# A hybrid decoder layer in one kernel: moving pieces of streamed weights, the group norm and two parameter transposes in TensorE's order

## The chip, the cores and the metric

The kernel runs on one core of a Trainium2 chip. The metric is the device time of one execution in microseconds (us), the median of several executions. Before the change it is 406.03 us.

## What is computed

The reference is one decoder layer on 256 tokens of width 1024. Two mixers share one input projection: RWKV-7 time mixing (8 heads of 64, a recurrence over the tokens) and softmax attention (8 heads of 64; with 256 tokens its blocks come down to plain causal attention). Their outputs are projected, gated, added and projected again; then comes a gated MLP of width 2816.

```
h = rms_norm(x, norm1_g)
proj = h @ w_in                              # recurrence inputs, q/k/v, two gates
z = shifted mix of proj[..., :RWKV_IN] with the token before
y_a = rwkv7_time_mix(z, ...)                 # state = state*w + (state@a)b + v k ; y = state@r
                                             # then a group norm over each head, + bonus, * g
y_b = moba_attention(rope(rms(q)), rope(rms(k)), v)
x = x + (sigmoid(g_a) * (y_a @ w_branch_a) + sigmoid(g_b) * (y_b @ w_branch_b)) @ w_out
x = x + conv_ffn(rms_norm(x, norm2_g), w_up, conv_w, conv_b, w_down)
```

## The kernel before

All large products are done in split form: a weight tile arrives by DMA (`raw`), ScalarE rounds it to a high part (`whi`, L259), VectorE subtracts to get the low part (`wlo`, L269), and TensorE makes three products for each tile (high by high, high by low, low by high). In the input and branch projections (`wst`, L293) one *piece* is 12 such matmuls of 128x256 (L302, L304, L307) and two pieces use up one weight tile. There are three `wlo` buffers, so the next low part can be made when TensorE leaves a tile.

The recurrence works on four chunks of 64 tokens. Within a chunk the delta rule is a triangular system, whose inverse `X` is built from blocks of 16, then 32, then 64: `below` (L791) makes the off-diagonal products, `masked` (L797) masks them into `P`, `plain` (L808) and `turned_` (L818) multiply on, and VectorE adds the results to `X`. Then, chunk by chunk: products with the state (L933, L938), with the inverse (L946), the state update (L956) and the output `y` (L968). `group_norm` takes each chunk's `y`: sum and centring (L892 to L895), square (ScalarE, L896), variance (L898, L899), a power of -1/2 on GpSimd (L900), scaling (L903), two full-size transposes on TensorE into `pc` (L910), and four steps that give the high and low parts `yah` and `yal` (L915 to L918), which the branch projection of the recurrence, `branch(0, *yah)`, reads.

All of these small matmuls use a part of the 128x128 array (64x64, 64x128 or 128x64); streamed pieces and the `pc` transposes use all of it.

The order of the instructions is written by a small planner at the end of `body` (L1174 to L1189). Each thread is a generator: `chain` (recurrence), `gn` (group norm), `att` (attention) and `bulk` (streamed pieces). A thread issues instructions and then yields `(cost, latency)`: the planner's clock advances by the cost, and the thread is due again after the latency. At each step the first thread of the list that is due goes; so the list's order is the priority. `bulk` stands last, costs 1.32 for a piece and has no latency, so it fills whatever time the others leave. `group_norm` holds back its transposes until the last step with a cost was not one of `bulk` (`joined`), so they stand next to other small matmuls. Beyond the threads, after `bulk` has ended, only `branch(0, *yah)`, the output projection and the MLP follow. On VectorE and ScalarE the compiler may let a later instruction go first when an earlier one is not ready by its own estimate; TensorE's order in the trace is the planner's.

The two parameter tables `p1` (51 rows) and `p2` (88 rows) come in by DMA as rows and are turned by TensorE into columns (L158, L1249).

Of the kernel before, what the change touches and what calls it, by code (L numbers as in the profile page):

```python
# [18 lines left out]
S = 256  # L19
# [18 lines left out]
def body(tc, x, positions, norm1_g, w_in, rwkv_mu, w_decay_up, decay_bias, w_aaa_up,  # L38
# [3 lines left out]
    act, dve, pool, pe = nc.scalar, nc.vector, nc.gpsimd, nc.tensor  # L42
    ctx = ExitStack()
    with ctx:
# [19 lines left out]
        def t1(name, shape=(128, 256), dt=F32):  # L64
            return sb.tile(list(shape), dt, name=name, tag="c1", bufs=8)
# [4 lines left out]
        def acc(name="acc"):  # L70
            return ps.tile([128, 512], F32, name=name, tag="acc", bufs=3)

        def chp(name="ch"):
            return ps.tile([128, 512], F32, name=name, tag="ch", bufs=3)

        def atp(name="at"):
            return ps.tile([128, 512], F32, name=name, tag="at", bufs=2)
# [14 lines left out]


        p0 = t1("p0", (8, 128))
        p1 = t1("p1", (51, 128))
        mu1 = rwkv_mu[0]
        rk1 = r_k[0].rearrange("h n -> (h n)").rearrange("(n c) -> n c", c=128)

# [14 lines left out]
        ident = cst.tile([128, 128], F32, name="ident")  # L113
# [41 lines left out]

        def late_params():
            pt = atp("pt")
            pe.transpose(pt[:, 0:51], p1, ident[:51, :51])  # L158
            dve.tensor_copy(par[:, 8:59], pt[:, 0:51])
            dve.tensor_scalar(omm, par[:, MU:MU + 15], -1.0, 1.0, op0=OP.mult, op1=OP.add)  # L160
            dve.tensor_scalar(omka, par[:, KA:KA + 4], -1.0, 1.0, op0=OP.mult, op1=OP.add)
# [60 lines left out]
        def load_next(first=False, into=None):  # L222
            if queue:
                ap = queue.pop(0)
                raw = wp.tile([128, 1024], F32, name="raw", tag="raw", bufs=NRAW) if into is None else into
                if ap is None:

                    nc.sync.dma_start(raw[:, 0:CW], w_gate_up[0, 0:128])
                    for r in range(4):
                        nc.sync.dma_start(raw[32 * r:32 * r + 32, CW:2 * CW], w_gate_up[0, 128:160])  # L230
                    raws.append((raw, 2, CW))
                    return
                k, c = ap.shape[1], ap.shape[2]
                rv = raw[:, :k * c].rearrange("p (k c) -> p k c", k=k)
                for ks in ((slice(0, 2), slice(2, 4)) if first else (slice(0, k),)):
                    nc.sync.dma_start(rv[:, ks], ap[:, ks])
                raws.append((raw, k, c))
# [126 lines left out]
        def first_steps():  # L364
# [5 lines left out]
            for t in early:  # L370
                for i in range(2):
                    load_next(into=t[:, i])
            dve.memset(ones, 1.0)
            dve.memset(eps1[:, 0:1], NORM_EPS)
            dve.memset(eps1[:, 1:2], GN_EPS)
            keep_warm(8)
# [10 lines left out]
            pt = atp("pt")  # L387
# [67 lines left out]
            p = acc()  # L455
# [29 lines left out]
        with tc.manual_schedule(engines={E.PE, E.Activation, E.DVE, E.Pool}):  # L485
            p = first_steps()
# [24 lines left out]
        p = acc()  # L511
# [39 lines left out]
        def need(nm, d):  # L551
            while nm not in d:
                yield 0, 0.5
# [6 lines left out]
        def chain():  # L560
# [36 lines left out]
            p = [chp("pss") for _ in range(2)]  # L597
            for t in range(2):
                for ct in range(4):
                    i = 4 * t + ct  # L600
# [14 lines left out]
            for j in range(2):  # L615
                p = chp("prx").rearrange("p (a t c) -> p a t c", a=2, t=2)
# [163 lines left out]
            def zeros():  # L780
                P = [b2("P", [128, 8, 64]) for _ in range(2)]
                for t in P:
                    pool.memset(t, 0.0)
                return P
# [10 lines left out]
            def masked(P, p, mk, w):  # L795
                m = level(0, w, mk[:, None, :])
                dve.tensor_tensor(level(0, w, P), p, m.to_broadcast([128, 8, 32 // w, w]), op=OP.mult)  # L797
# [38 lines left out]
            for j in range(2):  # L836
                p, pg = chp(), chp("pg")
# [21 lines left out]
            pp = below(16)  # L859
            for q in range(2):  # L860
                masked(P[q], pp[q], m16, 16)
            yield 1.1, 2.0
            P2 = zeros()
            px = plain(P, 16)
            pt = turned_(0, P[0], 16)
# [5 lines left out]
            pt = turned_(1, P[1], 16)  # L871
# [4 lines left out]
            pt = [turned_(q, P2[q], 32) for q in range(2)]  # L876
# [8 lines left out]
            def group_norm():  # L885

                for c in range(4):
                    yield from need(c, ny)
                    y = ny[c]
                    cs = slice(64 * c, 64 * c + 64)  # L890
                    st = sb.tile([128, 3, 4], F32, name="st", tag="st", bufs=2)
                    dve.tensor_reduce(st[:, 0], y, axis=AX.X, op=OP.add)  # L892
                    dve.tensor_scalar(st[:, 0], st[:, 0], -1.0 / N, None, op0=OP.mult)
                    yc, sq2 = t1("yc", (128, 4, 64)), t1("sq2", (128, 4, 64))
                    dve.tensor_tensor(yc, y, st[:, 0][:, :, None].to_broadcast([128, 4, 64]), op=OP.add)  # L895
                    act.activation(sq2, yc, AF.Square)  # L896
                    yield 0, 0.8
                    dve.tensor_reduce(st[:, 1], sq2, axis=AX.X, op=OP.add)  # L898
                    marks.append(dve.tensor_scalar(st[:, 1], st[:, 1], N * GN_EPS, None, op0=OP.add))  # L899
                    pool.tensor_tensor(st[:, 2], st[:, 1], mhalf, op=OP.pow)  # L900
                    yield 0, 1.6
                    with tc.issue_after(zadds[0].ins if c == 0 and zadds else marks[-1].ins):
                        dve.scalar_tensor_tensor(yc, yc, math.sqrt(N), st[:, 2][:, :, None].to_broadcast([128, 4, 64]),  # L903
                                                 op0=OP.mult, op1=OP.mult)
                    yield 0, 1.2 if c < 3 else 2.2
                    while not joined[0] and "chain" not in done:
                        yield 0, 0.1
                    p = chp("pc").rearrange("p (a n) -> p a n", a=8)
                    for j in range(2):
                        pe.transpose(p[:, 2 * j:2 * j + 2].rearrange("p a n -> p (a n)"),  # L910
                                     yc[:, 2 * j:2 * j + 2].rearrange("p q n -> p (q n)"), ident)
                    if c == 3:
                        settle(p.rearrange("p a n -> p (a n)"))
                    yf = t1("yf", (128, 4, 64))
                    dve.tensor_tensor(yf, p[:, 0:4], A1[:, :, cs], op=OP.mult)  # L915
                    dve.tensor_tensor(yf, yf, A2[:, :, cs], op=OP.add)
                    act.copy(yah_[:, :, cs], yf)
                    dve.tensor_tensor(yal[:, :, cs], yf, yah_[:, :, cs].bitcast(F32), op=OP.subtract)  # L918
                    yield 0.5, 2.0

            threads.insert(1, ["gn", group_norm(), 0.0])
            joined[0] = True
            St = None
            for c in range(4):
# [56 lines left out]
        marks = []  # L981
# [32 lines left out]
        def attention():  # L1014
            qkT = []
            for i in range(2):
                dT = b4(f"qkT{i}")
                p = [atp("pqk").rearrange("p (a t c) -> p a t c", a=4, t=2) for _ in range(2)]
# [44 lines left out]
            def normed(i, behind, also):  # L1063
                t, j, nh, sc = parts[i]
                with tc.issue_after(behind.ins), tc.issue_after(also.ins):
                    dve.reciprocal(sums[i], sums[i])
                    dve.tensor_tensor(sc, sc, sums[i][:, :, None].to_broadcast([128, nh, 128 * (t + 1)]), op=OP.mult)
# [29 lines left out]

            for i, part in enumerate(parts):
                scores(*part)
                yield 0.9, 4.7 if i == 1 else 5.0  # L1100
                most = softmax(*part)
                if i == 1:
                    normed(0, most, most)
# [6 lines left out]
            weighted(0, p0)  # L1110
            pa = turned_w(*parts[1])
            yield 1.8, 2.0
            normed(2, marks[1], zadds[0])
            yield 0, 1.0
            pb = turned_w(*parts[2])
# [59 lines left out]
        threads = [["chain", chain(), 0.0], ["bulk", bulk(), 0.0]]  # L1175
# [14 lines left out]

        x_sb = load_x()

        p2 = t1("p2", (88, 128))
        nc.gpsimd.dma_start(p2[0:66], conv_w[0].rearrange("w (n c) -> (w n) c", c=128))
        nc.gpsimd.dma_start(p2[66:88], rows(conv_b, 22))
        mhl += [sb.tile([128, 8, S], F32R, name=n, tag="b8", bufs=5) for n in ("mh", "ml")]
# [41 lines left out]
        def token_scale():  # L1238

            rx = t1("rx2", (128, 2, 128))  # L1240
            p = chp("prs")
            for t in range(2):
                dve.tensor_reduce(rs[:, t:t + 1], ss[:, t], axis=AX.X, op=OP.add)
            act.activation(rs, rs, AF.Sqrt, scale=1.0 / D, bias=eps1[:, 0:1])
            dve.reciprocal(rs, rs)
            dve.tensor_copy(rx, rs[:, :, None].to_broadcast([128, 2, 128]))
            for t in range(2):
                pe.transpose(p[:, t * 128:t * 128 + 128], rx[:, t], ident)
            pe.transpose(p[:, S:S + 88], p2, ident[:88, :88])  # L1249
            act.copy(rsb, p[:, 0:S])  # L1250
            act.copy(cpar, p[:, S:S + 88])

# [123 lines left out]
```

## Time and profile before

| what | us |
|---|---|
| median of 3 runs | 406.03 |
| lowest, highest | 405.90, 407.27 |
| span of the profiled execution, first to last instruction | 403.9 |
| what lies around the span, taken as median less span | 2.1 |
| TensorE busy | 396.4 |
| VectorE busy | 324.6 |
| ScalarE busy | 233.9 |
| share of the 16 DMA engines' time in the main queue | 57.1% of the span |

Busy time is the union of an engine's instructions. Matmuls overlap one another in their pipeline, so a busy TensorE isn't the same as one at its peak, but an idle one has surely waited. The granted TensorE clock is at its full level (2.4 GHz) in every slice.

### The profile page before, as it was taken

Reading aid. Unit: us, or ns where it says so; the run is one execution under the profiler, and the core shown is the slowest. Engines: PE = TensorE matmul, PEld = TensorE weight load, DVE = VectorE, ACT = ScalarE, POOL = GpSimd, SP = SyncE. Lnnn points to the kernel's source line nnn. Section 1 sums busy time; section 2 is a strip of 40 time slices with the busy share of each in tenths; the row PEclk is TensorE's granted clock in tenths of the full one; section 3 lists DMA queues with packets and bytes.
Section 4 is the critical chain, followed back from the end, with each engine's and each line's share of the span. In section 5 each row is a group of like instructions: output and inputs, shape, how many; then the busy total and the mean of one; then the engine's idle time right before and its main releaser. Section 6 shows DMA issues by size and latency. Waiting matters only on the chain.

```text
span 403.9 us, 8280 instructions
## 1 busy us (share of the span) xinstructions
PE 396.4 (98%) x3250; PEld 348.7 (86%) x3250; DVE 324.6 (80%) x574; ACT 233.9 (58%) x397; POOL 41.8 (10%) x69
## 2 busy tenths in 40 slices
PE   7999999999989999999999999999999999999996
PEld 3999989788989989999888888888888888888885
DVE  3988999899667978778965898977869778687694
ACT  6799755475647676444563784655546446355440
POOL 7910070010500011020011000000000000000000
PEclk9999999999999999999999999999999999999999
DMA  8954555564783444536563756676665665656612
GB/s 243 317 168 154 160 161 158 160 176 150 159 220 104 115 150 131 183 112 207 191 183 97 242 157 208 181 232 189 200 204 163 208 187 177 207 174 209 196 48 104
DMA packets 61990, 70.53 MB, mean 175 GB/s; under 512 B 9421, under 2 KB 52243, under 8 KB 61952
## 3 DMA queue, kind: packets, MB, share of 16 engines
q1 hardware_dynamic: 61104, 69.54, 57.1%
q0 software_dynamic: 832, 0.47, 0.6%
q8 instruction: 25, 0.41, 0.5%
q14 instruction: 13, 0.11, 0.1%
q10 hardware_dynamic: 16, 0.00, 0.0%
HBM read 68.56 MB, written 1.44 MB: 173 GB/s over the span
## 4 chain that ended last, share of the span: by engine, by line
PE 93%; DVE 2%; ACT 1%; DMA 1%; issue 1%; SPq 0%; POOL 0%; DVEq 0%; POOLq 0%; ACTq 0%
PE acc L1262 15%; PE acc L302 9%; PE acc L304 8%; PE acc L307 8%; PE acc L1267 8%; PE at L1262 5%; PE acc L323 5%; PE acc L327 5%; PE acc L324 5%; PE f L1286 5%; PE f L1282 5%; PE f L1284 4%; PE at L1267 3%; PE acc L461 1%; DMA x<-in_x_dram 1%; PE pgr L682 1%
## 5 line engine op out<-in xcount | busy, mean ns | idle before, releaser
L259 ACT CAST whi<-raw 128x1024 fp32r<-128x1024 f32 x120 | 125.7, 1051 | 106.0 <-PE acc L1262 22.2
L269 DVE TENSOR_TENSOR wlo<-raw,whi 128x1024 fp32r<-128x1024 f32 x121 | 148.8, 1234 | 26.2 <-PE acc L1267 12.2
L1262 PE MATMUL acc<-hx,whi 128*128 128x512 f32 x264 | 68.2, 393 | 0.0
L302 PE MATMUL acc<-hx,whi 128*128 128x256 f32 x232 | 58.3, 287 | 0.0
L304 PE MATMUL acc<-hx,whi 128*128 128x256 f32 x232 | 55.9, 277 | 0.0
L1262 PEld LDWEIGHTS acc<-hx,whi 128*128 128x128 f32 x264 | 47.0, 188 | 8.1
L302 PEld LDWEIGHTS acc<-hx,whi 128*128 128x128 f32 x232 | 43.6, 188 | 2.0 <-issue 0.8
L304 PEld LDWEIGHTS acc<-hx,whi 128*128 128x128 f32 x232 | 43.6, 188 | 0.1
L1267 PEld LDWEIGHTS acc<-h,wlo 128*128 128x128 f32 x264 | 37.1, 188 | 3.6
L1267 PE MATMUL acc<-h,wlo 128*128 128x256 f32 x264 | 37.8, 279 | 0.0
L307 PE MATMUL acc<-hx,wlo 128*128 128x256 f32 x232 | 35.7, 277 | 0.0
L1284 PE MATMUL f<-whi,hb 128*128 128x512 f32 x80 | 31.2, 390 | 0.0
L1286 PE MATMUL f<-wlo,hb 128*128 128x512 f32 x80 | 31.2, 390 | 0.0
L1282 PE MATMUL f<-whi,hb 128*128 128x512 f32 x80 | 31.2, 389 | 0.0
L307 PEld LDWEIGHTS acc<-hx,wlo 128*128 128x128 f32 x232 | 30.6, 188 | 0.0
L1262 PE MATMUL at<-hx,whi 128*128 128x512 f32 x88 | 24.0, 392 | 0.0
L1272 DVE TENSOR_REDUCE an<-acc 128x256 f32<-128x512 f32 x22 | 14.2, 685 | 9.3 <-PE acc L1267 9.3
L1262 PEld LDWEIGHTS at<-hx,whi 128*128 128x128 f32 x88 | 16.4, 188 | 3.6
L323 PE MATMUL acc<-whi,hx 128*128 128x512 f32 x48 | 19.1, 399 | 0.0
L324 PE MATMUL acc<-whi,hx 128*128 128x512 f32 x48 | 18.8, 391 | 0.0
L1286 PEld LDWEIGHTS f<-wlo,hb 128*128 128x128 f32 x80 | 15.0, 188 | 3.2
L1284 PEld LDWEIGHTS f<-whi,hb 128*128 128x128 f32 x80 | 15.0, 188 | 2.8
(331 smaller groups left out, 688.5 us busy)
## 6 DMA issues: line engine op xcount, KB each, us to landing
raw<-in_w_ffn_up_dram SPq DMA_DIRECT2D x44, 512.0 KB, 4.3
raw<-in_w_in_dram SPq DMA_DIRECT2D x37, 512.0 KB, 4.3
raw<-in_w_ffn_down_dram SPq DMA_DIRECT2D x22, 512.0 KB, 4.0
raw<-in_w_out_dram SPq DMA_DIRECT2D x8, 512.0 KB, 4.1
x<-in_x_dram SPq DMA_DIRECT2D x8, 256.0 KB, 4.4
early<-in_w_in_dram SPq DMA_DIRECT2D x4, 512.0 KB, 7.6
raw<-in_w_branch_b_dram SPq DMA_DIRECT2D x4, 512.0 KB, 3.4
raw<-in_w_branch_a_dram SPq DMA_DIRECT2D x4, 512.0 KB, 3.5
```

Of the source, the lines that this page charges most:

```text
L259: act.copy(wide(hi, k, c), spread(raw, k, c))
L269: eng.tensor_tensor(wide(lo, k, c), spread(raw, k, c), wide(hi, k, c).bitcast(F32), op=OP.subtract)
L302: pe.matmul(om, wh[:, k, ms], xh[:, k0 + k], start=k0 + k + m == 0, stop=False, skip_group_check=True)
L304: pe.matmul(om, wh[:, k, ms], xl[:, k0 + k], start=False, stop=False, skip_group_check=True)
L307: pe.matmul(om, wl[:, k, ms], xh[:, k0 + k], start=False, stop=k0 + k == nk - 1 and m == n - 1, skip_group_check=True)
L323: pe.matmul(ps_[t], xh[:, K, ts], wh[:, k], start=K == 0, stop=False)
L324: pe.matmul(ps_[t], xl[:, K, ts], wh[:, k], start=False, stop=False)
L1262: pe.matmul(ps_[m], wh[:, k, m * 128:m * 128 + 128], hx[:, k0 + k].rearrange("p a s -> p (a s)"), start=k0 + k == 0, stop=False, skip_grou ...
L1267: pe.matmul(ps_[m][:, 0:S], wl[:, k, m * 128:m * 128 + 128], h2[k0 // 4][:, k], start=False, stop=k0 + k == 7, skip_group_check=True)
L1282: pe.matmul(fin[f], hb[:, 0, i, ts], wh[:, 0, cs], start=st, stop=False, skip_group_check=f == 3)
L1284: pe.matmul(fin[f], hb[:, 1, i, ts], wh[:, 0, cs], start=False, stop=False, skip_group_check=f == 3)
L1286: pe.matmul(fin[f], hb[:, 0, i, ts], wl[:, 0, cs], start=False, stop=False, skip_group_check=f == 3)
```

## The change

Four edits. In `chain`, the wait that the planner allows after the first masks grows from 2.0 to 2.6. The thread `gn` is put into the list just ahead of `bulk` instead of second, so that it stands behind `att` in priority; `att` also gets a longer latency after its first scores (6.4 instead of 5.0) and a loop that waits, in the planner, until two variances have been issued. `p1` and `p2` are made 128 rows high, cleared by a memset first, and turned with the whole identity. The list of `gn`'s last latency is written otherwise with the same values.

```diff
-        p1 = t1("p1", (51, 128))
+        p1 = t1("p1", (128, 128))
...
-            pe.transpose(pt[:, 0:51], p1, ident[:51, :51])
+            pe.transpose(pt[:, 0:128], p1, ident)
...
             dve.memset(ones, 1.0)
+            dve.memset(p1, 0.0)
...
                 masked(P[q], pp[q], m16, 16)
-            yield 1.1, 2.0
+            yield 1.1, 2.6
...
-                    yield 0, 1.2 if c < 3 else 2.2
+                    yield 0, (1.2, 1.2, 1.2, 2.2)[c]
...
-            threads.insert(1, ["gn", group_norm(), 0.0])
+            threads.insert(len(threads) - 1, ["gn", group_norm(), 0.0])
...
                 scores(*part)
-                yield 0.9, 4.7 if i == 1 else 5.0
+                yield 0.9, (6.4, 4.7, 5.0)[i]
...
             yield 1.8, 2.0
+            while len(marks) < 2:
+                yield 0, 0.1
             normed(2, marks[1], zadds[0])
...
-        p2 = t1("p2", (88, 128))
+        p2 = t1("p2", (128, 128))
+        pool.memset(p2, 0.0)
...
-            pe.transpose(p[:, S:S + 88], p2, ident[:88, :88])
+            pe.transpose(p[:, S:S + 128], p2, ident)
```

## Rows read from the trace of the kernel before

**Rows 1.** The page: each engine's busy time; queue 8, which loads instructions.

```profile
PE 396.4 (98%) x3250; PEld 348.7 (86%) x3250; DVE 324.6 (80%) x574; ACT 233.9 (58%) x397; POOL 41.8 (10%) x69
...
q8 instruction: 25, 0.41, 0.5%
```

**Rows 2.** Two of TensorE's waits, whole span: total us, times, longest us.

```profile
PE px L808 <- issue: 1.1, 1, 1.1
PE pc L910 <- DVE yc L903: 0.6, 1, 0.6
```

**Rows 3.** Timeline around the inverse's first masks: start us, us, engine, line.

```profile
116.12 0.76 DVE L797 TENSOR_TENSOR P<-pp,m 128x256 f32<-128x256 f32 x2 [2.15 <-PE pp L791]
...
118.83 0.82 PE L808 MATMUL px<-P,X 64*64 64x32 f32 x41
...
120.70 0.49 PE L808 MATMUL px<-P,X 64*64 64x32 f32 x20 [1.05 <-issue]
```

**Rows 4.** DMA queues in the window 118 to 119.4 us.

```profile
q1 hardware_dynamic: 488, 0.48, 102.3%
q8 instruction: 1, 0.02, 5.3%
```

**Rows 5.** One window: its us, then each engine's busy us (x instructions).

```profile
120.65:125.45 4.80, 4.75 (x128) 4.54 (x128) 3.78 (x8) 2.53 (x8) 0.00 (x0) 1.00 0.37 119
```

**Rows 6.** Timeline at the first chunk's norm transposes.

```profile
146.94 0.41 PE L910 MATMUL pc<-ident,yc 128*128 128x128 f32 x2 [0.63 <-DVE yc L903]
```

**Rows 7.** Timeline of the streamed pieces and the last chunk, on TensorE.

```profile
172.23 0.69 PE L968 MATMUL pb<-VU,G 128*64 128x64 f32 x16
...
176.60 0.62 PE L307 MATMUL acc<-ybh,wlo 128*128 128x256 f32 x4
177.96 0.62 PE L307 MATMUL acc<-ybh,wlo 128*128 128x256 f32 x4
...
179.77 0.38 PE L910 MATMUL pc<-ident,yc 128*128 128x128 f32 x2
...
180.34 0.39 PE L302 MATMUL acc<-ybh,whi 128*128 128x256 f32 x1
...
183.58 0.19 PEld L304 LDWEIGHTS acc<-yal,whi 128*128 128x128 f32 x1 [0.16 <-DVE yal L918]
```

**Rows 8.** Timeline of the last chunk's norm on the other engines.

```profile
178.07 0.43 DVE L903 SCALAR_TENSOR_TENSOR yc<-yc,st 128x256 f32<-128x256 f32 x1 [1.18 <-POOL st L900]
...
180.15 0.68 DVE L1138 SCALAR_TENSOR_TENSOR gt<-gt,acc 128x512 f32<-128x512 f32 x1
...
180.75 0.41 DVE L915 TENSOR_TENSOR yf<-pc,A 128x256 f32<-128x256 f32 x1
...
181.08 1.21 DVE L269 TENSOR_TENSOR wlo<-raw,whi 128x1024 fp32r<-128x1024 f32 x1
...
182.21 0.41 DVE L916 TENSOR_TENSOR yf<-yf,zr 128x256 f32<-128x256 f32 x1
...
183.10 0.42 DVE L918 TENSOR_TENSOR yal<-yf,yah 128x256 fp32r<-128x256 f32 x1 [0.47 <-ACT yah L917]
```

**Rows 9.** Timeline: the second chunk's transposes and the step behind them.

```profile
157.48 0.44 PE L910 MATMUL pc<-ident,yc 128*128 128x128 f32 x2
...
157.95 0.42 DVE L915 TENSOR_TENSOR yf<-pc,A 128x256 f32<-128x256 f32 x1 [0.18 <-PE pc L910]
```

**Rows 10.** Timeline: the turning of p1, a memset of that size, DVE's first work.

```profile
16.40 0.26 PE L158 MATMUL pt<-ident,p 51*128 51x51 f32 x1
16.59 0.38 PE L302 MATMUL acc<-hx,whi 128*128 128x256 f32 x1
16.82 0.28 PE L304 MATMUL acc<-hx,whi 128*128 128x256 f32 x1
...
16.42 0.20 POOL L130 MEMSET bones<- 128x128 f32 x1
...
4.20 0.15 DVE L399 TENSOR_SCALAR ss<-ss 128x1 f32<-128x1 f32 x1 [2.64 <-ACT xn L396]
```

## The prediction

> **What bounds the kernel now.** I read the page first: TensorE is busy for 396.4 of 403.9 us, the others far less [rows 1]. So TensorE's order and its holes decide, and a piece of work that merely changes place on it costs nothing. The next view is the list of TensorE's waits. Beyond the start-up, in which the input arrives, it has two entries: 1.05 us before a matmul of L808, put down to no engine ("issue"), and 0.63 us before the first chunk's norm transposes, put down to VectorE's scaling L903 [rows 2, 6]. A third, 0.16 us, is seen in the timeline where the last branch product begins and waits for the low part `yal` [rows 7]. That is the ceiling: with 0.2 us for `p1` (below), an order without any hole would save about 2.0 us, 0.5%, of which a run can just tell. New holes have no such ceiling.
>
> The timeline then shows what the first hole is. The masks were ready at 116.88; the products that read them began at 118.83, ran 41 matmuls, stopped at 119.65 and went on at 120.70 with nothing else ending then [rows 3]. What does fall there is a load of instructions: queue 8 made 25 loads of 16.4 KB in the run, one for some 260 of TensorE's 6,500 instructions [rows 1], and one of them lies between 118 and 119.4, while weights took 102% of the DMA engines [rows 4]. Tiny matmuls use up code fast: 256 instructions in the 4.8 us behind the hole [rows 5], against 24 for a piece of 1.36 us. I take the hole for late code.
>
> The Trainium skill (Runtime: NRT & Kernel Launch, Instruction fetch mechanics) says that the sequencer fetches the next 16 KiB block of 256 instructions while it executes the current one, and that crossing a boundary is mostly hidden. By that rule the hole would not be code and the first gain below would be in doubt, 408.4 in place of 407.4; this trace shows 1.05 us that wasn't hidden.
>
> **The change, part by part.** *One more piece behind the first masks.* In the planner `below` goes at 92.58 and ends at 93.68; `plain` was due at 95.68, scores ran to 94.58 and one piece to 95.90. Due at 96.28 instead, it lets a second piece in. Followed on, with the longer latency of the scores, the chain keeps the same spacing up to the first norm transposes: two pieces between the steps as before, just one piece further in the stream. So only this place changes. The code load was asked for earlier, by instructions that don't move; while it arrives TensorE now has a piece of 1.36 us [rows 7], then some 100 instructions of `plain` that are already there. That is more than 1.05 us. The gain is between 0 (the hole moves to another dense stretch) and 1.3 us (hole and pipeline refill); I take 1.05, the row's own value.
>
> *The first norm transposes.* The order before them is the same: output of chunk 0, two pieces, products with the state, a piece, attention's transposes, the next inverse product, `pc`. Of VectorE's steps only the relative priority changes. The 0.63 us [rows 6] may vanish or double; I take no change.
>
> *The norm behind attention.* This is the costly part. The thread gets its turn only when attention isn't due, and must still catch a step that isn't `bulk` before its transposes. In the planner the second chunk's transposes fall from 131.2 to 139.6, the third's from 142.8 to 150.6. The last chunk's output goes at 146.8 (145.9 before), but its sum, centring and square are issued only at 153.7, the variance at 155.1, and `bulk` runs out of pieces at 156.4. The scaling comes at 156.7, the transposes at 158.9. Before, they stood at 153.7, ahead of the last two pieces. Now they stand behind them, and the next product on TensorE, the recurrence's branch, reads exactly what they lead to. Nothing can fill that gap: the output projection and all else depend on this product.
>
> Its price: before, from the start of the last transposes to the end of `yal` took 3.75 us (179.77 to 183.52), in which a branch result (0.68) and a low part (1.21) went ahead on VectorE [rows 7, 8]. It was hidden but for 0.16 us by two pieces of 1.36. Without such company the chain is 0.47 from transposes to the first step [rows 9], then four steps of 0.41 with small gaps: 2.25 us [rows 8]. Of either, TensorE works 0.57 on the transposes and the settling matmuls behind them (179.77 to 180.34) and 0.12 on a first matmul that needs only `yah` [rows 7]. The hole is thus at least 1.6 us and 3.1 with the same company. The last branch result surely goes ahead, for it is ready when the pieces end, 0.4 us before the transposes are; so at least 2.1. A low part is free at the same moment, because a `wlo` buffer is. I take 2.8, less the 0.16 that goes away: 2.6.
>
> Late scaling would add to it. Before, the scaled value was ready at 178.50, 6.3 us after the last output began [rows 7, 8]. Now six pieces, the output and the third chunk's transposes, some 9.2 us, lie in between; but the steps are issued later and behind two low parts and two branch results on VectorE. Up to one low part, 1.2 us, may still be in front: the upper end is 4.3.
>
> *Parameters.* The 51-row transpose uses a part of the array between full-size products: 0.19 us to the next matmul and 0.23 to the one after, where 0.12 is the pace [rows 10]. At full size I take 0.2 off; the ends are 0 and 0.3. The 88-row one takes the whole array's width anyway: 0. The memsets are some 0.2 us each, by one of 128x128 on GpSimd [rows 10]. The one on VectorE falls into its idle 2.64 us before 4.2 [rows 10], and the loads that wait for it are GpSimd's own, issued after other work; uncovered, 0.2. The one on GpSimd is far ahead of its use, but may stand in front of the last power: 0.2, inside the upper end. The new loop of attention never waits: two variances are out by 129.7, and it comes at 131.0.
>
> **Sum.** 403.9 - 1.05 - 0.2 + 2.6 = 405.25, and with 2.1 around the span 407.4. That is 1.3 us over the median, 0.3%: under the 0.5% (2.0 us) that a measurement of this kernel can tell.
>
> **Rivals.** *Slower: the norm is late as well.* The last scaling isn't ready when the pieces end, because VectorE takes low parts and branch results first. The hole is 4.3 instead of 2.8: 408.9. It decides from a scaling some 0.7 us behind the last piece. For it: VectorE is busy for 80% [rows 1], and it did let a low part in between two norm steps [rows 8]. Against: 9.2 us are there for 6.3 us of work.
>
> *The first hole only moves,* to the next stretch of tiny matmuls, as code is used up there just as fast [rows 5], or was no code: 405.25 + 1.05 + 2.1 = 408.4. Against: the piece stands exactly ahead of the place, and the load then comes in time.
>
> *Nothing lost.* VectorE is free when the transposes come, the hole is 1.6, and the first chunk's 0.63 vanishes: 403.9 - 1.05 - 0.2 - 0.63 + 1.45 + 2.1 = 405.6, no change. Faster by 0.5%, under 404.0, needs a last chunk without a hole; the order speaks against that.
>
> **Numbers.** Forecast 0.50 (its own range 406.4 to 408.2), late norm 0.20, moved hole 0.13, nothing lost 0.17. Slower by over 0.5% is from 408.06: all of the first rival, most of the second, a little of the forecast: 0.36. Faster: 0.04. Range: from 405.0, under the third rival, to 409.8, a late norm and a moved hole together with some re-ordering.
>
> **What would show it.** Right: no idle time on TensorE inside L808; idle time of 2 to 4 us put down to `yf`, `yah` or `yal` ahead of the first matmul with `yah`, with the last `pc` behind all `ybh` pieces; L158 followed at 0.12. Wrong: `pc` of the last chunk ahead of a piece, or the 0.63 grown past 1.5 us, or a fall of the granted clock in the new hole, whose price no row here shows.

## The result and the profile after

The changed kernel takes 411.29 us, the median of five runs (410.73 to 412.58), against 406.03 for the five of the kernel before beside it (405.71 to 407.37): 1.0131 times as long, 95% interval 1.0096 to 1.0166. The forecast was 407.4 with a range up to 409.8, so the change cost far more than I had worked out, and on the side that I had thought of second. The granted clock averages 0.992 of full speed in the two longest executions (412.21 and 412.58) and 0.996 in the three others (410.73 to 411.29).

The profiled execution is the longest of the five: 412.58 us, span 410.8, 6.9 more than the span before; its sums below are thus some 1.3 us more than the median's. On the page, TensorE's busy time grew by 3.4 us for the same 3250 matmuls, and the row of the granted clock, which was at its full level in all 40 slices before, has a 6 in slice 19 [rows 1 are the same line of before]:

```profile
PE 399.8 (97%) x3250; PEld 352.2 (86%) x3250; DVE 324.8 (79%) x575; ACT 233.9 (57%) x397; POOL 42.1 (10%) x70
...
PEclk9999999999999999996999999999999999999999
```

TensorE's waits name the places (total us, times, longest us). The entry put down to "issue" at the first masks [rows 2] is gone; two long ones and one of 0.7 are new (of the 1.7 at `pc`, 0.5 is the first chunk's wait [rows 6], 1.2 is new):

```profile
PE acc L302 <- ACT yah L918: 2.4, 1, 2.4
PE pc L911 <- DVE yc L904: 1.7, 2, 1.2
...
PE acc L302 <- ACT gt L1132: 0.7, 1, 0.7
```

Next, the timeline of TensorE at these places: the turned parameter rows, the first masks, the new wait, and the tail (start us, us):

```profile
16.61 0.27 PE L158 MATMUL pt<-ident,p 128*128 128x128 f32 x1
16.64 0.37 PE L302 MATMUL acc<-hx,whi 128*128 128x256 f32 x1
16.84 0.28 PE L304 MATMUL acc<-hx,whi 128*128 128x256 f32 x1
...
120.56 1.34 PE L809 MATMUL px<-P,X 64*64 64x32 f32 x63
...
132.75 0.38 PE L302 MATMUL acc<-hx,whi 128*128 128x256 f32 x1 [0.70 <-ACT gt L1132]
...
182.23 0.63 PE L307 MATMUL acc<-ybh,wlo 128*128 128x256 f32 x4
184.09 0.41 PE L911 MATMUL pc<-ident,yc 128*128 128x128 f32 x2 [1.23 <-DVE yc L904]
184.43 0.33 PE L559 MATMUL pc<-ident 64*64 64x64 f32 x4
187.19 1.01 PE L302 MATMUL acc<-yah,whi 128*128 128x256 f32 x3 [2.43 <-ACT yah L918]
```

The products with the first masks now run with hardly a stop: from the first of them to the next streamed matmul it takes 1.80 us (120.56 to 122.36), against 2.82 before [rows 3] (118.83 to 121.65). A gap of 0.2 is left behind the 28th of them; kernels below that have no gap take 1.53. In the tail the last piece ends its four L307 near 182.71 (182.23 and four steps of 0.12); with 0.57 for transposes and settling [rows 7] the branch with `yah` could begin at 183.28, and begins at 187.19: two holes of 3.9 us together. VectorE in the same stretch says why:

```profile
180.11 0.69 DVE L1141 SCALAR_TENSOR_TENSOR gt<-gt,acc 128x512 f32<-128x512 f32 x1
180.70 0.42 DVE L899 TENSOR_REDUCE st<-sq 128x4 f32<-128x256 f32 x1
181.03 1.22 DVE L269 TENSOR_TENSOR wlo<-raw,whi 128x1024 fp32r<-128x1024 f32 x1
182.16 0.17 DVE L900 TENSOR_SCALAR st<-st 128x4 f32<-128x4 f32 x1
183.52 0.43 DVE L904 SCALAR_TENSOR_TENSOR yc<-yc,st 128x256 f32<-128x256 f32 x1 [1.18 <-POOL st L901]
183.86 0.68 DVE L1141 SCALAR_TENSOR_TENSOR gt<-gt,acc 128x512 f32<-128x512 f32 x1
184.81 0.42 DVE L916 TENSOR_TENSOR yf<-pc,A 128x256 f32<-128x256 f32 x1 [0.27 <-PE pc L559]
185.15 1.22 DVE L269 TENSOR_TENSOR wlo<-raw,whi 128x1024 fp32r<-128x1024 f32 x1
186.28 0.42 DVE L917 TENSOR_TENSOR yf<-yf,zr 128x256 f32<-128x256 f32 x1
```

One low part stands between the two halves of the variance, and another between the two steps behind the transposes. The first takes about as long (1.22) as `pc` then waits for the scaling (1.23); the second lengthens the way from `pc` to `yah`.

The third loss is in the windows (us of the window, busy us of PE, PEld, DVE, ACT, POOL with instructions, granted clock, DMA share, GB/s):

```profile
183.00:186.30 3.30, 0.67 (x6) 0.40 (x6) 2.51 (x5) 0.52 (x1) 1.80 (x4) 1.00 0.51 179
186.30:193.20 6.90, 6.00 (x28) 6.01 (x29) 0.88 (x4) 1.26 (x2) 0.00 (x0) 0.51 0.23 77
193.20:196.50 3.30, 3.30 (x30) 3.30 (x30) 2.93 (x4) 1.17 (x3) 0.00 (x0) 1.00 0.19 14
```

TensorE had been idle for most of the 4.5 us up to 187.2. From about 186.3 to 193.2 it was granted 0.51 of its speed, the lower level of 1.2 GHz: 28 matmuls in 6.9 us, then 30 in 3.3.

From the start of the output projection to the end the kernels shown here differ by less than 0.1 us (209.5 to 209.6), so all of the loss lies ahead of that start: 194.36 us before, 201.28 after.

### The profile page after: what moved, and what is told of

It reads as the page before. It is cut to its first block, busy times and chain, and to the rows that moved or that the text cites. A ratio compares the mean times of both kernels' runs of the same rounds, so it can differ in the third digit from the quotient of the medians.

```text
span 410.8 us, 8285 instructions
## 1 busy us (share of the span) xinstructions
PE 399.8 (97%) x3250; PEld 352.2 (86%) x3250; DVE 324.8 (79%) x575; ACT 233.9 (57%) x397; POOL 42.1 (10%) x70
## 4 chain that ended last, share of the span: by engine, by line
PE 91%; DVE 4%; DMA 1%; ACT 1%; issue 1%; POOL 1%; SPq 0%; DVEq 0%; POOLq 0%; ACTq 0%
PE acc L1266 15%; PE acc L302 9%; PE acc L307 8%; PE acc L304 8%; PE acc L1271 7%; PE at L1266 5%; PE acc L323 5%; PE acc L327 4%; PE f L1288 4%; PE acc L324 4%; PE f L1286 4%; PE f L1290 4%; PE at L1271 2%; PE acc L462 1%; DVE wlo L269 1%; DMA x<-in_x_dram 1%
## 5 line engine op out<-in xcount | busy, mean ns | idle before, releaser
L307 PE MATMUL acc<-hx,wlo 128*128 128x256 f32 x232 | 35.8, 277 | 0.0
L307 PEld LDWEIGHTS acc<-hx,wlo 128*128 128x128 f32 x232 | 30.7, 188 | 0.1
```

Of the source, the lines that this page charges most:

```text
L307: pe.matmul(om, wl[:, k, ms], xh[:, k0 + k], start=False, stop=k0 + k == nk - 1 and m == n - 1, skip_group_check=True)
```

## The experiments

All kernels ran beside the kernel before on the same chip; ratios are to it, with 95% intervals. Each has a name, given with its result. Times of places are from one profiled execution of each kernel.

### The norm's thread put back

```diff
-            threads.insert(len(threads) - 1, ["gn", group_norm(), 0.0])
+            threads.insert(1, ["gn", group_norm(), 0.0])
```

> The changed kernel with one line undone: the norm's thread stands second again, ahead of attention; the rest of the change stays. Theory (the loss is the norm's place, through the tail): the fall of the granted clock at 186 us goes (-3.0), the two tail holes of together 4.0 us shrink to one of at most 1.7, because by the planner the last transposes now have one streamed piece of 1.36 us behind them instead of none (and two in the kernel before): 3.75 from transposes to the low part, less 1.36, 0.57 and 0.12. The hole at the first masks stays away; the new 0.7 us wait for ScalarE's gate evacuation stays. Span near 410.8 - 3.0 - 2.3 = 405.5, time 407 to 408. Rival 1 (the loss is spread over the stream: the slower pace of the pieces, the new wait, the late start): time stays over 409.5. Rival 2 (a hole of 1.7 us already costs the clock): the clock still falls, time about 410.5.

Measured (norm_second_again): 406.05 us, ratio 1.0008 (0.9992 to 1.0024). The one line carries nearly the whole loss. No window of the tail is below full clock, and TensorE's waits are:

```profile
PE acc L302 <- ACT gt L1132: 0.7, 1, 0.7
...
PE px L809 <- issue: 0.4, 1, 0.4
PE acc L302 <- ACT yah L918: 0.2, 1, 0.2
```

The time is 1 to 2 us better than expected, because the tail hole is 0.2 and not up to 1.7: `pc` starts at 181.90 and `yah` is there at 184.32, 2.4 us later, since the low part on VectorE had begun (181.82) before the transposes did and no branch result came between; one piece covers nearly all of it. But a part of the hole at the masks has come back, 0.4 us.

### The norm's move alone

```diff
-            threads.insert(1, ["gn", group_norm(), 0.0])
+            threads.insert(len(threads) - 1, ["gn", group_norm(), 0.0])
...
+            while len(marks) < 2:
+                yield 0, 0.1
             normed(2, marks[1], zadds[0])
```

> The kernel before with only the norm's thread moved behind attention, and attention's loop that needs it; no longer latency behind the masks or the scores, old parameter rows. Theory: all of the loss comes with this one line. Two holes ahead of the recurrence's branch of together 4.0 us less the 0.16 of before, and a stretch at half clock worth 3.0: span 403.9 + 6.8 = 410.7, the hole of 1.05 at the first masks is still there; time 412 to 414, so a little slower than the changed kernel. Rival (the loss needs the other edits): time at most 409.

Measured (norm_behind_alone): 409.26 us, ratio 1.0088 (1.0064 to 1.0111). Neither number was right: the move alone loses 3.5 us, not 6 to 8. Here the scaled value is in time (`pc` follows the last piece at 182.72 without a wait), and one hole is left:

```profile
185.89 0.62 PE L302 MATMUL acc<-yah,whi 128*128 128x256 f32 x3 [2.54 <-ACT yah L917]
```

Its clock falls too, but for half as long:

```profile
186.00:187.00 1.00, 1.00 (x8) 0.96 (x9) 0.30 (x1) 0.00 (x0) 0.00 (x0) 1.00 0.60 115
187.00:190.60 3.60, 3.60 (x20) 3.60 (x20) 0.00 (x0) 0.39 (x1) 0.00 (x0) 0.53 0.30 114
```

This is the forecast's own hole (2.8 worked out). The late scaling joins it only in the changed kernel, which has the extra piece at the masks, attention's longer latency and the parameter rows besides; which of them makes the scaling late was not tried. In four executions of this kernel the mean clock is 0.996 twice and 0.999 to 1.0 twice: with a hole of this size the fall doesn't come each time. In all five of the changed kernel it is 0.992 to 0.996.

### Filling the holes

```diff
+                    if c == 3:
+                        fill = chp("fill")
+                        for _ in range(5):
+                            pe.matmul(fill, ones[:, 0:128], ones, start=True, stop=True)
                     p = chp("pc").rearrange("p (a n) -> p a n", a=8)
...
                         settle(p.rearrange("p a n -> p (a n)"))
+                        for _ in range(11):
+                            pe.matmul(fill, ones[:, 0:128], ones, start=True, stop=True)
```

> The changed kernel with 16 matmuls of 128x512 (bf16, of ones, into a bank that nobody reads) in the tail's two holes: 5 between the last piece and the last norm transposes, 11 behind the settling matmuls; they need nothing and are shorter than the holes at 0.21 us each. Theory (the clock fell because TensorE stood idle): the holes stay as long for the work that matters, but the granted clock stays at 2.4 GHz, and the span falls by the 3.0 us that the half clock cost: 407.8, time 408 to 409. Rival (the clock falls for another reason, or the half clock costs nothing since the weights are late anyway): no fall of the time, 411; with the clock restored and no gain, the weights were the bound there.

Measured (filled_tail): 408.98 us, ratio 1.0084 (1.0056 to 1.0113), so some 2 us less than the changed kernel. The same work with `yah` starts at nearly the same time as there (187.44 against 187.19), at full clock:

```profile
183.00:187.00 4.00, 3.82 (x22) 1.84 (x23) 2.92 (x5) 1.02 (x2) 2.27 (x4) 1.00 0.63 186
187.00:190.50 3.50, 3.44 (x27) 2.89 (x26) 0.43 (x1) 0.40 (x2) 0.00 (x0) 1.00 0.51 150
```

From there to the output projection it takes 11.75 us (to 199.19), in the changed kernel 14.09: the half clock cost 2.3 us there. The weights were there, so they weren't the bound. Matmuls that compute nothing win back over a third of the loss (2.3 of 5.3 us by the medians).

```diff
                         settle(p.rearrange("p a n -> p (a n)"))
+                        fill = chp("fill")
+                        for _ in range(11):
+                            pe.matmul(fill, ones[:, 0:128], ones, start=True, stop=True)
```

> The changed kernel with 11 matmuls of 128x512 (bf16, of ones, into a bank that nobody reads) behind the settling matmuls alone; the first of the tail's two holes (1.4 us, the wait for the scaled value) stays empty. Theory (it is the idle time of both holes together, some 4 us within 4.6, that brings the clock down): with only 1.4 us left idle the granted clock stays full and the time is that of filled_tail, 409. Rival (the first hole alone is enough): a stretch at half clock remains, 410 to 411.

Measured (filled_second_hole): 409.48 us, ratio 1.0086 (1.0062 to 1.011), the same as with both filled. The hole ahead of `pc` stays, and behind it the products with `yah` run at full clock (the trace has records of 10 of the 11 matmuls):

```profile
183.98 0.41 PE L911 MATMUL pc<-ident,yc 128*128 128x128 f32 x2 [1.22 <-DVE yc L904]
184.32 0.33 PE L559 MATMUL pc<-ident 64*64 64x64 f32 x4
184.59 2.55 PE L917 MATMUL fill<-ones 128*128 128x512 bf16 x10
187.08 0.62 PE L302 MATMUL acc<-yah,whi 128*128 128x256 f32 x3
```

So the first hole of 1.2 us, left alone, brings no fall of the clock here. That it takes both holes, as the theory had it, isn't shown: the second was never left empty alone in this kernel, and norm_behind_alone, with one hole of 2.54 us, has the fall too.

### Behind attention, but without the pause after each chunk

```diff
-                    yield 0.5, 2.0
+                    yield 0.5, 0
```

> The changed kernel, with the norm's thread still behind attention, but its latency of 2.0 after each chunk's transposes set to 0: by the planner the last chunk's sum comes 5.3 us sooner, and its transposes with one piece behind them instead of none. Theory (what costs is that the last chunk's steps are issued too late for a piece to be left, not the place behind attention as such): the tail is that of norm_second_again, a hole of 0.3 us, full clock, and the time is 406 to 406.5. Rival (the norm behind attention costs elsewhere too, on VectorE or in the first chunks): over 408.

Measured (norm_sooner): 406.82 us (405.66 to 409.53 in ten executions), ratio 1.0023 (0.9998 to 1.0048). The last transposes stand at 181.95 with a piece behind them again, and the clock stays full in the tail:

```profile
PE px L809 <- issue: 0.7, 1, 0.7
PE acc L302 <- ACT gt L1132: 0.7, 1, 0.7
PE acc L302 <- ACT yah L918: 0.6, 1, 0.6
```

The priority behind attention isn't the price in itself, though two of the ten executions lie over the rival's 408 (408.59 and 409.53), at a mean clock of 1.0; no trace of them was kept. The thread takes its chunks one after another and pauses for 2.0 after each, so what attention delays in the second and third chunk arrives undiminished at the fourth, where no piece is left. The time is a little over the 406 to 406.5 expected. In the profiled execution (407.78) the hole at the masks came back with 0.7 us, and the hole of the tail is 0.6, not 0.3.

### The piece behind the masks alone

Here the kernel before gets the latency 2.6 and attention's 6.4, and nothing else (the diff has both lines).

> The kernel before with the one more piece behind the first masks and the longer latency of attention's first scores, nothing else. Theory: the holes at the first masks go (1.05 by the row, 1.3 with the refill, another 0.2 in the next dense stretch), but the piece that hides them is missing at the end: only one stands behind the last norm transposes, so up to 1.7 us come back there; and a wait of 0.7 for the gate evacuation comes in. Span 403.9 - 1.5 + 1.5 + 0.7 = 404.6, time 406 to 407.5: no gain. Rival (the missing piece costs nothing, the first hole is a gain): time 404.5 or less.

Measured (masks_piece_alone): 405.54 us, ratio 0.9998 (0.9984 to 1.0012), the theory's "no gain". The hole at the masks is gone, and these two are in its place:

```profile
PE acc L302 <- ACT gt L1129: 0.7, 1, 0.7
...
PE acc L302 <- ACT yah L917: 0.2, 1, 0.2
```

From the first of the products with the masks to the next streamed matmul it takes 1.53 us (120.24 to 121.77), 1.29 less than before. The missing piece at the end costs 0.2, far less than the 1.7 allowed for; the gate wait is the larger of the two waits that eat the gain.

### The gate wait

```diff
-            def turned_(q, P, w):
+            def turned_(q, P, w, fs=(chp, acc)):
 
-                p = [half_bank("px", w, f) for f in (chp, acc)]
+                p = [half_bank("px", w, f) for f in fs]
...
-            pt = [turned_(q, P2[q], 32) for q in range(2)]
+            pt = [turned_(q, P2[q], 32, (chp, (acc, chp)[q])) for q in range(2)]
```

> The changed kernel with the norm's thread second again and one more edit: of the two products turned_(q, P2[q], 32), the second takes both its banks from the pool ch, none from acc. Theory (the new 0.7 us wait is a lack of acc banks: two of three are taken by turned_ at the moment when the next gate product wants one, and the third is still being emptied by ScalarE): the wait for the gate evacuation goes and the kernel gains 0.7 us on norm_second_again, 406.05 to 405.35, ratio to before 0.999. Rival (the wait moves to the products with ch, whose third bank isn't free either): no gain, ratio 1.001.

Measured (norm_second_banks): 405.19 us, ratio 0.998 (0.996 to 1.0001). Behind the start, TensorE's list has two small waits left, that of before at the first transposes and that of the tail:

```profile
PE pc L911 <- DVE yc L904: 0.5, 1, 0.5
PE acc L302 <- ACT yah L918: 0.2, 1, 0.2
```

The wait for `gt` was a lack of banks, then: it goes when one product takes its bank elsewhere. (The time can't show the 0.7 us: the interval reaches 1, and the hole of 0.4 at the masks is missing in this execution too.) In the changed kernel the evacuation (L1132) stood among attention's exponentials (L1059) on ScalarE, and TensorE's next gate product had to sit them out:

```profile
131.63 0.49 ACT L1059 ACTIVATE sc<-sc,mx 128x256 f32<-128x256 f32 x1
132.03 0.19 ACT L1059 ACTIVATION_READ_ACCUMULATOR sc<-sc,mx 128x1 f32 x1
132.12 0.58 ACT L1132 ACTIVATE gt<-acc 128x512 f32<-128x512 f32 x1
```

### Last transposes earlier, and old parameter rows

> As norm_second_banks, and the norm's last chunk may send its transposes after 1.2 in place of 2.2, so that by the planner two streamed pieces stand behind them again. Theory: the tail hole of 0.3 us that norm_second_again has goes to 0.1, since the scaled value was ready over 1 us before its turn; with the hole at the first masks and the gate wait gone, 404.9 to 405.2, ratio 0.997 to 0.999. Rival (the transposes now wait for the scaling): no gain on norm_second_banks.

Measured (mended): 405.43 us, ratio 0.9971 (0.995 to 0.9992). The tail's hole at `yah` is gone, but the transposes wait as the rival said:

```profile
179.83 0.41 PE L911 MATMUL pc<-ident,yc 128*128 128x128 f32 x2 [0.76 <-DVE yc L904]
```

> The kernel before with one more piece behind the first masks, attention's longer latency, the banks of ch and the earlier last transposes, but with the old parameter rows (51 and 88) and their transposes. Theory: what masks_piece_alone lost to the gate wait (0.7) and the tail (0.3) is gained: 404.6, ratio 0.9975. Against mended it shows what the parameter rows do in company: theory within 0.3 us, rival 0.5 us less without them.

Measured (mended_small_params): 405.25 us, ratio 0.9978 (0.996 to 0.9997). The rows make no difference that these intervals can tell. By the ratio norm_second_banks, mended and mended_small_params are at 0.2 to 0.3% less than the kernel before; they can't be told from one another. Most of this lies in the granted clock of the kernel before: in eight of its 35 executions beside these kernels it averaged 0.994 to 0.996, and they took 407.25 to 408.48 us. The median of the other 27 is 405.58, and the three kernels, with one such execution in 36, have medians of 405.19 to 405.43. Where the clock fell in those eight isn't known, as no trace of them was kept; that the hole at the masks brought it down is open.

> The kernel before with only the two parameter tables at 128 rows, their memsets and their full-size transposes. Theory (forecast): at most 0.2 us gained behind the first transpose and nothing elsewhere, ratio 0.999 to 1.000. Rival (the changed kernel's start, 0.37 us late by 39 us, comes from here: a memset on VectorE in the start, a larger transpose): ratio 1.001.

Measured (params_alone): 405.86 us, ratio 0.9989 (0.9968 to 1.001). The 0.2 us at the transposition is there in the trace (below), the time can't show it. That the changed kernel's start is late because of the rows isn't borne out by these runs.

### The hole at the masks: code or data

```diff
             keep_warm(8)
+            for _ in range(8):
+                pe.matmul(idle[:, 0:64], ones[:, 0:128], ones[:, 0:64], start=True, stop=True)
```

> The kernel before with 8 more matmuls of 128x64 on ones at its very start, where TensorE waits for the input anyway: 16 more instructions (a weight load and a matmul each) ahead of everything else, and no other difference. Theory (the hole at the first masks is late code, at a fixed count of TensorE's instructions): the hole moves 8 matmuls nearer to the start of the 64 small products, from behind the 41st to behind the 32nd to 33rd, and lasts about as long, 0.8 to 1.1 us. Rival (it is a wait for data or for a bank): it stays behind the 40th or 41st.

One execution (code_shift), 409.11 us, span 407.3. The hole stands behind the 33rd product instead of the 41st, 8 matmuls earlier, as the theory said:

```profile
120.34 0.71 PE L810 MATMUL px<-P,X 64*64 64x32 f32 x33
122.64 0.61 PE L810 MATMUL px<-P,X 64*64 64x32 f32 x28 [1.60 <-issue]
```

It is longer, 1.6 instead of 1.05, and here too the clock falls behind it:

```profile
122.00:123.60 1.60, 0.96 (x63) 0.95 (x62) 1.56 (x3) 1.04 (x1) 0.00 (x0) 1.00 0.90 198
123.60:127.20 3.60, 3.60 (x27) 3.56 (x21) 2.56 (x8) 1.36 (x2) 0.00 (x0) 0.53 0.40 137
```

Data and banks would have stayed with their matmul. The same reading explains norm_second_again and norm_sooner: their hole stands behind the 28th product instead of the 41st, 12 or 13 matmuls earlier (a record may be missing), and the piece ahead adds 24 instructions, 12 of them matmuls.

The traces show more: when the load of queue 8, which brings instructions [rows 1], began at that moment. In us from the start, by the packets of that queue, with the time from the first product to the next streamed matmul in the last column:

| kernel | load begins | load is over | products begin | TensorE goes on | takes |
|---|---|---|---|---|---|
| before | 118.13 | 119.32 | 118.83 | 120.70 | 2.82 |
| code_shift | 120.00 | 121.10 | 120.34 | 122.64 | 3.36 |
| norm_sooner | 119.36 | 120.49 | 120.54 | 121.92 | 2.55 |
| norm_second_again | 119.45 | 120.52 | 121.02 | 122.06 | 2.21 |
| changed kernel | 118.61 | 119.70 | 120.56 | 121.19 | 1.80 |
| norm_second_banks | 117.95 | 119.05 | 120.06 | no gap | 1.53 |

Wherever there is a gap, TensorE goes on 1.4 to 1.55 us after the load is over; that holds in params_alone, norm_behind_alone and filled_second_hole (a gap of 0.1) as well, eight kernels in all. In the five without a gap (filled_tail, masks_piece_alone, norm_second_banks, mended and mended_small_params) the load is over 1.4 to 2.2 us ahead of the 29th product. The load itself takes 0.9 to 1.2 us in all 13. So the wait is for code, and how much of it is left goes with the time at which the load begins. What TensorE still waits for in those 1.4 us isn't shown.

## Why the prediction was wrong

**The step that failed** is the term of the norm behind attention: "I take 2.8", with the last scaling in time and the granted clock at nothing. The runs show 3.9 us of holes in its place, since the scaling was late, and 2.3 us of half clock behind them. The other terms follow in the order of the prediction.

**The hole at the masks: right, the number with some luck.** The first streamed matmul behind these products starts at 122.36, against 121.65 before, with one piece of 1.36 and 0.37 of late start more ahead of it: 1.02 us gained, 1.05 forecast, and 0.15 more in the next dense stretch. Without the gap that is left it would have been the 1.29 of masks_piece_alone, the forecast's upper end. That it is late code is now shown by the shifted count and by the loads. The Trainium skill (Runtime: NRT & Kernel Launch, Instruction fetch mechanics) calls crossing a block of 256 instructions mostly hidden. With one wait for 25 loads [rows 1, 2] that holds over the run, but not at this place, with 0.8 to 1.6 us in the kernels without the piece. The gain isn't safe either: of the nine profiled kernels with two pieces ahead of these products, two kept a hole, of 0.4 and 0.7, and two a gap of 0.1 to 0.2. I had the load asked for by instructions that don't move, so at a fixed place in the stream. It began at 117.4 to 118.1 in the five kernels without a gap, at 118.6 and 118.9 in the two with a small one, and at 119.4 and 119.5 in the two with a hole. Why it begins earlier or later stays open.

**"So only this place changes": wrong, by 0.7 us.** I followed the order of the pieces and not the banks. With one more piece ahead, the two products `turned_` with blocks of 32 come directly behind the end of a gate and take two of the three `acc` banks while ScalarE still has to empty the third. masks_piece_alone has the wait, norm_second_banks removes it.

**The first norm transposes: right.** 0.5 us of wait against 0.63 [rows 6].

**The norm behind attention: the order right, the size wrong.** The order came as followed: the last transposes behind all pieces, `yf`, `yah` and `yal` in the open. Of the sizes, "I take 2.8" holds for the way from the last piece to `yah` when the scaling is in time: norm_behind_alone waits 2.54. In the whole change the scaling is late as well, which I had as a rival with 0.20 and an upper end of 4.3; measured are 3.9 (above). I argued against it that 9.2 us were there for 6.3 of work. But the steps were issued late: in the trace the variance's reduction runs at 180.70, only 2.0 us ahead of the end of the last piece, with a low part right behind it. norm_sooner shows the cause: with the steps issued sooner, the last transposes come ahead of the last piece and find the scaled value ready.

**The granted clock: not in the sum.** I named it as what would make the prediction wrong, and gave it no price as the trace of before had no fall in it. It costs 2.3 us in the profiled execution, by filled_tail, and less in the median one, whose mean clock is 0.996 and not 0.992. That stretch of 96 `yah` products runs at a pace of 0.118 us per matmul in filled_tail (and in the changed kernel from 193.2 on), against 0.113 in most of the kernel before. In filled_second_hole it runs at 0.113 and takes 11.12 us (187.08 to 198.20). Against 11.75 another 0.6 lies in the pace.

**Parameters: right.** Transposition to the second matmul behind it: 0.23 us at full size (16.61 to 16.84), 0.42 before [rows 10]; 0.2 forecast. params_alone repeats it:

```profile
16.51 0.27 PE L158 MATMUL pt<-ident,p 128*128 128x128 f32 x1
...
16.74 0.28 PE L304 MATMUL acc<-hx,whi 128*128 128x256 f32 x1
```

**The sum of the profiled execution:** 3.9 (holes) + 2.3 (clock) + 0.6 (pace) + 0.7 (banks) + 0.4 (late start) - 1.2 (masks) - 0.16 (the old wait for `yal`, now within the hole) = 6.5 of the 6.9 us. The rest of 0.4 I can't place. The late start (117.62 against 117.25 for the same piece) differs from execution to execution: the products with the first masks begin at 120.06 in norm_second_banks and at 121.02 in norm_second_again, which have the same instructions up to there.

## What to carry to other kernels

Work that fills holes is a stock: a piece moved ahead to hide one wait, or a thread moved back, is paid at the end, where the stock runs out, so follow the order to the last piece and ask there what the next product needs and who stands in front of it on each engine. A hole of some microseconds on TensorE can cost again by a lower granted clock behind it; where nothing useful was left to run, products that nobody reads won back about 2 us here. When a wait looks like late code, read when the load began and ended, and compare kernels. When a step moves next to another, follow the banks and the engine that empties them, not just the order.

## What was not expected of the hardware

The granted clock fell behind quite different stretches: 3.7 us of idleness in two parts (0.51 for 6.9 us), one hole of 2.54 (0.53 for 3.6 us), and a hole of 1.6 us among products of 64x64 (0.53 for 3.6 us). It did not fall behind 1.2 us between full-size pieces with fillers behind it (filled_second_hole), nor behind the 1.05 us at the masks in the profiled execution of the kernel before.

In the stretches read here, streamed 128x256 matmuls run at one of two paces, 0.113 or 0.118 us from start to start, at full clock. The pace changes at islands of small products and holds until the next: with the same instructions, the stretch from 22.85 to the next streamed product at 40.20 (17.35 us) in the kernel before takes 17.97 in filled_tail (22.67 to 40.64). What chooses the pace wasn't tried, and stays open.
